# Attention stage: VectorE's instructions kept in the order in which the program issues them

## Chip, cores and metric

One core of a Trainium2 chip (trn2). The time is the device time of one execution in microseconds (us), as the median of several runs; all other times are from one execution that the hardware profiler recorded.

## What is computed

The kernel runs two blocks, one behind the other, on x of shape (1, 512, 1024) in float32. The first mixes a gated MLP branch and a chunked linear recurrence and ends with a feed-forward; the second has a short-convolution mixer with a feed-forward, then attention with another feed-forward. The change is in the attention: 16 heads of 64, 512 positions, causal, with a forget gate whose cumulative sum c is added to the scores. Cut to what matters:

```python
kvf = h @ w_kvf
k = rmsnorm_2(k_s, k_norm)                  # per head
c = cumsum(log_sigmoid(f_logit))
qg = xn @ b_w_qg[j]
q = rmsnorm_2(qg[..., :d], q_norm[j])       # per head
s = q . k + c[q] - c[k], causal             # 64 wide
o = softmax(s) @ v
o = o * sigmoid(qg[..., d:])
x = x + o @ b_w_out[j]
```

## The kernel before

Activations lie as eight tiles of 128 features by 512 positions. Every float32 product is split: each operand has a rounded part h and a remainder l, and three matmuls are summed (xh by wh at L207, xl by wh at L211, xh by wl at L212). A weight chunk is loaded raw by SyncE's queue, and `prep` (L173) makes wh on ScalarE (a cast, L183) and wl on VectorE (L184) up to two chunks ahead of use.

The order on each engine is made by a scheduler from its own estimate of times, not by the program: an instruction moves ahead of others that wait. Only an instruction given to `keep_in_program_order` (short name `pin`, L68) keeps its place among its engine's instructions; before the change those are a few matmuls and the first wl.

The attention stage runs two generators side by side, `weave(main(), side(), *ATT, late=True)` (L1462), which takes steps from one or the other by the amount of matmul work that each has issued. Four of the eight pairs of heads have their query's product issued before that.

- `main()` follows `ORDER = "gqgqgqgqgggg"`: each q is `query(i)`, a product of eight matmul triples and the start of a `HeadNorm`; each g is `gate(i)`: a product, then gz on VectorE (a multiplication by the norm factor rb, then a maximum with -80), then `clamp_sig` on ScalarE (e, e, sg: Exp, Ln, Exp). `paced` calls `finish_norms` and `start_norms` at the fourth and seventh step of each product.
- `HeadNorm.sums` (called by `start_norms`) sums squares on TensorE (L1224, L1225, into hn), then issues in this order: hm on VectorE; Ln and Exp into hr on ScalarE; hn times the gain times hr, on VectorE (L109); then hr by hr and hm by hr, on VectorE for the first four queries and on GpSimd for the later ones (`by`). `out` (called by `finish_norms`) ends it with one more instruction on VectorE.
- `side()` goes through 32 steps, eight pairs of heads by four row blocks tb of 128. A step issues `scores` (TensorE into sc, then two maxima nmx on VectorE, L1366), `shares` of the step before (rs, a reciprocal on VectorE, L1381, then pe times rs for both heads of the pair, L113, on GpSimd for tb 0 and 1, on VectorE for tb 2 and 3), `turn` of two steps before (transposes of pe into pt on TensorE, L1390, and a copy to et on ScalarE), `powers` (pe by Exp with a running sum, on ScalarE), and parts of `stack` (kh, kl, qh, ql of the next pair). Once all four row blocks of a pair are turned, `values` (ao on TensorE, L1403) and og, the gated output, follow a step later. `split` then makes xh and xl of og for the output product.

The lines that matter for the order within a HeadNorm:

```python
ts(dve, self.m, ps, 1.0 / 64, ALU.mult, EPS, ALU.add)
r = T("hr")
f(r, self.m, AF.Ln)
f(r, r, AF.Exp, scale=-0.5)
stt(self.t, self.t, self.gk, r, ALU.mult, ALU.mult)
```

Of the kernel before, what the change touches and what calls it, by code (L numbers as in the profile page):

```python
# [55 lines left out]
@with_exitstack  # L56
def tile_two_blocks(ctx: ExitStack, tc: tile.TileContext, a: dict, out: bass.AP):
    nc = tc.nc
    act, dve, pool, pe = nc.scalar, nc.vector, nc.gpsimd, nc.tensor

    cp = ctx.enter_context(tc.tile_pool(name="const", bufs=1))
    rawp = ctx.enter_context(tc.tile_pool(name="raw", bufs=N_RAW))
# [27 lines left out]
    def close_x():  # L90
        xp[0].close()
# [122 lines left out]
    def mm_T(key, X, m=128):  # L214
        wh, wl = W(key)
        ps = PS("mm")
        nk = len(X)
        o = ps[:m, :]
        for k in range(nk):
            mm3(o, wh[:, k, :], wl[:, k, :], X[k][0], X[k][1], k == 0, k == nk - 1)  # L220
            yield 650
        return ps
# [34 lines left out]
    def run(gen):  # L257
        try:
            while True:
                next(gen)  # L260
        except StopIteration as e:
            return e.value

    def weave(main, side, mt, st, late=False):

        m = s = 0.0
        end = object()
        md = sd = False
        while not (md and sd):
            c = None  # L270
            if not sd and (md or s * mt < m * st or late and not s):
                c = next(side, end)
                if c is end:
                    sd = True
                    continue
                if c is not None:
                    s += c
                    continue
                assert not md
            c = next(main, end)  # L280
            if c is end:
                md = True
            elif s or not late:
                m += c
# [206 lines left out]
    class Acc:  # L491
        def __init__(self):
            self.t = None
# [11 lines left out]
    def split(src, g=None, alloc=None):  # L505
        h, l = (alloc or R)("xh"), (alloc or R)("xl")
        if g is None:
            act.copy(h, src)  # L508
            tt(dve, l, src, h.bitcast(F32), ALU.subtract)
        else:  # L510
            f(h, src, AF.Copy, scale=g)
            stt(l, src, g, h.bitcast(F32), ALU.mult, ALU.subtract)
        return h, l
# [153 lines left out]
    def zi_half(c):  # L667
        pss = yield from mm_N("zi", X)
        for j in range(NT):
            v[j][c] = T("v")  # L670
            f(v[j][c], pss[j], AF.Copy, scale=rcol[:, j:j + 1])

    def head_in(h):
        kq, sc = T2("kq"), T2("sc")
        p = yield from mm_T("zf", X)
        t = T("zf")
        tt(dve, t, p, rb)
        e = T("e")
        f(e, t, AF.Abs)
        f(e, e, AF.Exp, scale=-1.0)  # L680
        f(e, e, AF.Ln, bias=1.0)
        g = T("g")
        stt(g, t, 0.0, e, ALU.min, ALU.subtract)
        dve.tensor_tensor_scan(out=sc[:, 1, :], data0=reset, data1=g, initial=0.0, op0=ALU.mult, op1=ALU.add)  # L684
        stt(e, t, 0.0, e, ALU.max, ALU.add)

        tt(pool, sc[:, 0, :], sc[:, 1, :], e, ALU.add)
        f(kq[:, 0, :], e, AF.Exp, scale=-1.0)
        p = yield from mm_T("zq", X)
        silu(p, kq[:, 1, :])  # L690
        heads[h] = (kq, sc)

    def gate_in(h):
        gate = T("gate")
        p = yield from mm_T("zo", X)
        silu(p, gate, hgs)
        gates[h] = gate
# [175 lines left out]
    def side():  # L873
        cores = {}
        ahead = [0]

        def look(upto):
            while ahead[0] < min(upto, 72):
                h, n = divmod(ahead[0], 9)
                if h not in cores:  # L880
                    if h not in heads:
                        return
                    cores[h] = Core(h)
                cores[h].decays(n)
                ahead[0] += 1

        for h in range(8):
            look(9 * h + 1)
            while h not in cores:
                yield None  # L890
                look(9 * h + 1)
            c = cores[h]
            look(9 * h + 5)
            if h == 0:
                for _ in range(HGSTART):
                    yield None
            c.small()
            look(9 * h + 9)
            yield 2000
            if h:  # L900
                cores[h - 1].values()
                cores[h - 1].square()
                yield 2200
            c.mid()
            yield 800
            if h:
                cores[h - 1].norm()
                yield 500
            c.far()
            look(9 * h + 9 + AHEAD)  # L910
            yield 2000
            if h:
                cores.pop(h - 1).done()
        cores[7].values()
        yield 1000
        cores[7].square()
        yield 1000
        cores[7].norm()
        yield 1000
        cores[7].done()  # L920
# [11 lines left out]
    def main():  # L932
        yield from zi_half(1)
        for h in range(1, 8):
            yield from head_in(h)
            yield from gate_in(h - 1)
        rest.extend(split(t) for t in YF)
        yield from gate_in(7)
        for i in range(N_FILL):
            yield from mix_a(i, rest)  # L940

    def mix_a(i, YA):
        pg = yield from mm_T("ga", X)
        py = yield from mm_T("ua", YA)
        t = T("m1")
        gated(pg, py, t)
        M1.append(t)
# [344 lines left out]
    def paced(mm):  # L1292

        n = 0
        while True:
            try:
                c = next(mm)
            except StopIteration as e:
                return e.value
            n += 1  # L1300
            if n == FIN:
                finish_norms()
            if n == START:
                start_norms()
            yield c

    def query(i):
        p = yield from paced(mm_T("qq", XQ))
        held.append((i, HeadNorm(p, kqs[:, 1:2], act if i < QL else pool)))
# [149 lines left out]
    turns = {"q": QL, "g": 0}  # L1459
    for i in range(QL):  # L1460
        run(query(i))
    weave(main(), side(), *ATT, late=True)  # L1462
    close_x()
    acc = Acc()
    X = [residual("bo", OS, i, V("ffn2", 8 + i), acc) for i in range(8)]
# [27 lines left out]
```

## Time and profile before

| | us |
|---|---|
| runs | 2096.36, 2099.39, 2098.18; median 2098.18 |
| profiled execution, its own time | 2099.46 |
| its span | 2097.7 |
| TensorE matmuls busy (PE) | 2054.9 (98%) |
| TensorE weight loads (PEld) | 1687.0 (80%) |
| VectorE (DVE) | 1180.5 (56%) |
| ScalarE (ACT) | 898.6 (43%) |
| GpSimd (POOL) | 466.4 (22%) |
| scores side by side with gates, from and to | about 1534 to 1690 of the span |

The span runs from the first to the last instruction; the execution's own time is 1.8 us longer. Busy times are of the whole span, so they say which engine is nearly always at work, and not what a single stage waits for; that is in the timelines of its stretch.

### The profile page before, as it was taken

How to read it: one execution, taken by the hardware profiler on the slowest of the kernel's cores; microseconds unless marked ns; L12 is line 12 of the kernel's file. 1: busy time of each engine (PE TensorE's matmuls, PEld its weight loads, DVE VectorE, ACT ScalarE, POOL GpSimd, SP SyncE). 2: the span in 40 equal slices, each digit the busy share in tenths (PEclk: the TensorE clock that was granted, in tenths of full speed). 3: DMA queues.
4: the chain of work that ended last, by engine and by line, in shares of the span. 5: the costliest groups of instructions: out<-in, count | busy, mean ns of one | idle time of the engine just before them, and what ended most of it. 6: DMA issues, size and time to landing. Idle time of an engine off the chain costs nothing.

```text
span 2097.7 us, 27515 instructions
## 1 busy us (share of the span) xinstructions
PE 2054.9 (98%) x11314; PEld 1687.0 (80%) x11314; DVE 1180.5 (56%) x1525; ACT 898.6 (43%) x1444; POOL 466.4 (22%) x421
## 2 busy tenths in 40 slices
PE   8999889999999999999999999999999999999999
PEld 7877678888888888888888888877877778888887
DVE  4678785555444443664654453567577566445353
ACT  5467675543322323522343232345566554323232
POOL 3546661012222222410210000120024211001000
PEclk9999999999999999999999999999999999999999
DMA  7131112323232233323333223241311113323221
GB/s 223 61 101 45 59 61 81 112 90 101 84 117 83 98 101 96 105 70 111 101 101 101 95 88 99 81 122 61 101 41 61 41 61 101 101 84 117 81 92 50
DMA packets 179190, 187.55 MB, mean 89 GB/s; under 512 B 4379, under 2 KB 169976, under 8 KB 179064
## 3 DMA queue, kind: packets, MB, share of 16 engines
q1 hardware_dynamic: 179048, 185.79, 27.4%
q8 instruction: 89, 1.46, 0.3%
q14 instruction: 37, 0.30, 0.0%
q10 hardware_dynamic: 16, 0.00, 0.0%
HBM read 183.68 MB, written 2.10 MB: 89 GB/s over the span
## 4 chain that ended last, share of the span: by engine, by line
PE 88%; DVE 4%; POOL 4%; ACT 2%; issue 1%; DMA 0%; SPq 0%; POOLq 0%; DVEq 0%; ACTq 0%
PE mm L207 26%; PE mm L211 26%; PE mm L212 26%; POOL dec L106 3%; PE mn L252 2%; PE mn L251 2%; PE mn L250 2%; PE sc L1354 1%; PE ao L1403 1%; DVE dec L106 1%; ACT e L119 1%; PE pt L1390 1%; PE ml L237 1%; PE ml L236 1%; PE ml L235 1%
## 5 line engine op out<-in xcount | busy, mean ns | idle before, releaser
L207 PE MATMUL mm<-xh,wh 128*128 128x512 f32 x2544 | 1001.9, 395 | 0.6 <-ACT xh L508 0.6
L211 PE MATMUL mm<-xl,wh 128*128 128x512 f32 x2544 | 993.9, 391 | 0.0
L212 PE MATMUL mm<-xh,wl 128*128 128x512 f32 x2544 | 992.8, 391 | 0.0
L183 ACT CAST wh<-raw 128x1024 fp32r<-128x1024 f32 (+2 forms) x354 | 363.8, 1028 | 787.5 <-PE mm L211 696.5
L184 DVE TENSOR_TENSOR wl<-raw,wh 128x1024 fp32r<-128x1024 f32 (+2 forms) x354 | 462.7, 1308 | 176.4 <-ACT wh L183 174.5
L207 PEld LDWEIGHTS mm<-xh,wh 128*128 128x128 f32 x2544 | 479.7, 189 | 102.3 <-ACT xh L508 0.8
L212 PEld LDWEIGHTS mm<-xh,wl 128*128 128x128 f32 x2544 | 479.4, 188 | 101.0 <-issue 0.2
L211 PEld LDWEIGHTS mm<-xl,wh 128*128 128x128 f32 x2544 | 479.7, 189 | 98.4 <-issue 0.3
L106 POOL TENSOR_TENSOR ua<-ua,rb 128x512 f32<-128x512 f32 x44 | 57.6, 1310 | 589.4 <-ACT ua L119 589.4
L106 DVE TENSOR_TENSOR x<-mm,x 128x512 f32<-128x512 f32 x64 | 44.2, 691 | 154.5 <-PE mm L212 154.5
L106 POOL TENSOR_TENSOR dec<-sc 128x256 f32<-128x256 f32 x96 | 78.8, 851 | 82.4 <-DVE sc L684 82.0
L106 POOL TENSOR_TENSOR acc<-acc,sq 128x512 f32<-128x512 f32 x42 | 67.0, 1596 | 105.0 <-ACT sq L119 77.9
L106 DVE TENSOR_TENSOR a<-mm,rb 128x512 f32<-128x512 f32 x44 | 30.4, 691 | 101.9 <-PE mm L212 101.6
L106 DVE TENSOR_TENSOR sg<-mm,ua 128x512 f32<-128x512 f32 x44 | 30.4, 692 | 92.6 <-POOL ua L106 90.1
L106 POOL TENSOR_TENSOR rl<-rl 128x512 f32<-128x512 f32 x32 | 48.1, 1502 | 117.0 <-ACT rl L119 117.0
L109 DVE SCALAR_TENSOR_TENSOR ua<-a,convs,ua 128x511 f32<-128x511 f32 x88 | 65.8, 748 | 4.7 <-ACT ua L119 3.2
L113 POOL TENSOR_SCALAR pe<-pe,rs 128x128 f32<-128x128 f32 (+1 forms) x32 | 29.6, 937 | 164.7 <-DVE rs L1381 160.5
L119 ACT ACTIVATE ua<-ua 128x512 f32<-128x512 f32 x44 | 27.8, 632 | 85.9 <-DVE ua L109 85.8
L250 PE MATMUL mn<-wh,xh 128*128 128x512 f32 x160 | 62.7, 398 | 0.0
L251 PE MATMUL mn<-wl,xh 128*128 128x512 f32 x160 | 62.4, 390 | 0.0
L252 PE MATMUL mn<-wh,xl 128*128 128x512 f32 x160 | 60.7, 390 | 0.0
L109 DVE SCALAR_TENSOR_TENSOR xl<-x,vecs,xh 128x512 fp32r<-128x512 f32 x40 | 56.1, 1404 | 4.2 <-ACT xh L119 4.0
(279 smaller groups left out, 1838.5 us busy)
## 6 DMA issues: line engine op xcount, KB each, us to landing
raw<-in_ffn_w_up_dram SPq DMA_DIRECT2D x44, 1024.0 KB
raw<-in_w_ff_dram SPq DMA_DIRECT2D x32, 1024.0 KB
raw<-in_w_in_dram SPq DMA_DIRECT2D x26, 1024.0 KB
raw<-in_ffn_w_down_dram SPq DMA_DIRECT2D x18, 1024.0 KB
raw<-in_a_w_in_dram SPq DMA_DIRECT2D x12, 1024.0 KB
raw<-in_w_kvf_dram SPq DMA_DIRECT2D x8, 1024.0 KB
raw<-in_b_w_qg_dram SPq DMA_DIRECT2D x8, 1024.0 KB
raw<-in_w_up_b_dram SPq DMA_DIRECT2D x4, 1024.0 KB
```

The costliest lines, as they stand in the source:

```text
L106: e.tensor_tensor(out=o, in0=i0, in1=i1, op=op)
L109: dve.scalar_tensor_tensor(out=o, in0=i0, scalar=s, in1=i1, op0=op0, op1=op1)
L113: e.tensor_scalar(out=o, in0=i, scalar1=s1, scalar2=None, op0=op0)
L119: act.activation(out=o, in_=i, func=func, scale=scale, bias=bias, **kw)
L183: act.copy(hi, src)
L184: ins = dve.tensor_tensor(out=lo, in0=src, in1=hi.bitcast(F32), op=ALU.subtract)
L207: ins = pe.matmul(ps, lhsT=lh, rhs=rh, start=start, stop=False)
L211: pe.matmul(ps, lhsT=lh, rhs=rl, start=False, stop=False)
L212: pe.matmul(ps, lhsT=ll, rhs=rh, start=False, stop=stop_)
L250: pe.matmul(pss[j], lhsT=xh[:, t0], rhs=wh[:, kk, :], start=(k + kk == 0), stop=False)
L251: pe.matmul(pss[j], lhsT=xh[:, t0], rhs=wl[:, kk, :], start=False, stop=False)
L252: pe.matmul(pss[j], lhsT=xl[:, t0], rhs=wh[:, kk, :], start=False, stop=(k + kk == nk - 1))
```

## The change

Four engines are wrapped in a class that passes every call on and, while an engine is in the set `strict`, gives the instruction to `keep_in_program_order`. VectorE (`dve`) is put into the set before the weave, and the set is emptied after it. All instructions and their operands stay as they are. In the orders below, every call through the wrapper has the line L70 in the changed kernel.

```diff
--- before.py
+++ after.py
@@ -56,7 +56,25 @@
 @with_exitstack
 def tile_two_blocks(ctx: ExitStack, tc: tile.TileContext, a: dict, out: bass.AP):
     nc = tc.nc
-    act, dve, pool, pe = nc.scalar, nc.vector, nc.gpsimd, nc.tensor
+
+    strict = set()
+
+    class InOrder:
+        def __init__(self, engine):
+            self.engine = engine
+
+        def __getattr__(self, name):
+            call = getattr(self.engine, name)
+
+            def issue(*args, **kw):
+                ins = call(*args, **kw)
+                if self in strict and name != "dma_start":
+                    tc.keep_in_program_order(ins)
+                return ins
+
+            return issue
+
+    act, dve, pool, pe = (InOrder(e) for e in (nc.scalar, nc.vector, nc.gpsimd, nc.tensor))
 
     cp = ctx.enter_context(tc.tile_pool(name="const", bufs=1))
     rawp = ctx.enter_context(tc.tile_pool(name="raw", bufs=N_RAW))
@@ -1459,7 +1477,9 @@
     turns = {"q": QL, "g": 0}
     for i in range(QL):
         run(query(i))
+    strict.add(dve)
     weave(main(), side(), *ATT, late=True)
+    strict.clear()
     close_x()
     acc = Acc()
     X = [residual("bo", OS, i, V("ffn2", 8 + i), acc) for i in range(8)]
```

How this moves VectorE's instructions is shown at three places. A row has the line, the operation, the output with its allocation numbers, the operands and the shape; the numbers tell tiles of one name apart.

VectorE around query 3 (hm_2078_12133 is its HeadNorm, gz_2083 and wl_2087 belong to a gate, nmx_2082 and nmx_2098 to scores, rs_2099 to shares), before:

```order
L115 TENSOR_SCALAR hm_2078_12133<-hn_2077_12130 128x512
L106 TENSOR_TENSOR gz_2083_12161<-mm_2076_12107,rb_1890_11221 128x512
L106 TENSOR_TENSOR kl_2095_12185<-hn_1905_11286,kh_2093_12183 128x512
L1366 TENSOR_REDUCE nmx_2098_12202<-sc_2096_12188 128x1
L1366 TENSOR_REDUCE nmx_2098_12202<-sc_2097_12189 128x1
L113 TENSOR_SCALAR gz_2083_12161<-gz_2083_12161 128x512
L1381 RECIPROCAL rs_2099_12208<-sum_2089_12177 128x2
```

The same place in the changed kernel, from the row behind hm_2078_12133:

```order
L70 SCALAR_TENSOR_TENSOR hn_2066_12087<-hn_2066_12087,kqs_11140,hr_2079_12135 128x512
L70 TENSOR_TENSOR hr_2079_12135<-hr_2079_12135 128x512
L70 TENSOR_TENSOR hm_2078_12133<-hm_2078_12133,hr_2079_12135 128x512
L70 TENSOR_REDUCE nmx_2082_12158<-sc_2080_12144 128x1
L70 TENSOR_REDUCE nmx_2082_12158<-sc_2081_12145 128x1
L70 TENSOR_TENSOR gz_2083_12161<-mm_2076_12107,rb_1890_11221 128x512
L70 TENSOR_SCALAR gz_2083_12161<-gz_2083_12161 128x512
L70 TENSOR_TENSOR wl_2087_12170<-raw_2059_12044,wh_2086_12169 128x1024
L70 TENSOR_TENSOR kl_2095_12185<-hn_1905_11286,kh_2093_12183 128x512
L70 TENSOR_REDUCE nmx_2098_12202<-sc_2096_12188 128x1
L70 TENSOR_REDUCE nmx_2098_12202<-sc_2097_12189 128x1
L70 RECIPROCAL rs_2099_12208<-sum_2089_12177 128x2
```

hn_2066 with its operand hr_2079, and the two multiplications behind it, now stand directly behind hm_2078 (they stood behind wl_2087 and later rows), and rs_2099 comes behind them and behind wl_2087.

VectorE around query 4 (hm_2173 and hn_2148 are its HeadNorm; rs_2185 and pe_2168, pe_2169 are shares), before:

```order
L1381 RECIPROCAL rs_2185_12536<-sum_2167_12447 128x2
L115 TENSOR_SCALAR hm_2173_12490<-hn_2172_12487 128x512
L1366 TENSOR_REDUCE nmx_2177_12512<-sc_2176_12499 128x1
L113 TENSOR_SCALAR pe_2168_12448<-pe_2168_12448,rs_2185_12536 128x384
L113 TENSOR_SCALAR pe_2169_12450<-pe_2169_12450,rs_2185_12536 128x384
L106 TENSOR_TENSOR gz_2178_12518<-mm_2155_12401,rb_1890_11221 128x512
L184 TENSOR_TENSOR wl_2183_12529<-raw_2181_12526,wh_2182_12528 128x1024
L1366 TENSOR_REDUCE nmx_2195_12569<-sc_2193_12555 128x1
L1366 TENSOR_REDUCE nmx_2195_12569<-sc_2194_12556 128x1
L113 TENSOR_SCALAR gz_2178_12518<-gz_2178_12518 128x512
L1381 RECIPROCAL rs_2196_12575<-sum_2190_12550 128x2
L109 SCALAR_TENSOR_TENSOR hn_2148_12387<-hn_2148_12387,kqs_11140,hr_2174_12492 128x512
```

And in the changed kernel:

```order
L70 TENSOR_SCALAR hm_2173_12490<-hn_2172_12487 128x512
L70 SCALAR_TENSOR_TENSOR hn_2148_12387<-hn_2148_12387,kqs_11140,hr_2174_12492 128x512
L70 TENSOR_REDUCE nmx_2177_12512<-sc_2175_12498 128x1
L70 TENSOR_REDUCE nmx_2177_12512<-sc_2176_12499 128x1
L70 TENSOR_TENSOR gz_2178_12518<-mm_2155_12401,rb_1890_11221 128x512
L70 TENSOR_SCALAR gz_2178_12518<-gz_2178_12518 128x512
L70 TENSOR_TENSOR wl_2183_12529<-raw_2181_12526,wh_2182_12528 128x1024
L70 RECIPROCAL rs_2185_12536<-sum_2167_12447 128x2
L70 TENSOR_SCALAR pe_2168_12448<-pe_2168_12448,rs_2185_12536 128x384
L70 TENSOR_SCALAR pe_2169_12450<-pe_2169_12450,rs_2185_12536 128x384
```

hn_2148 moves from the end of the piece to the place behind hm_2173; rs_2185 and its two pe, once at the head, now stand at the end, behind a gate and wl_2183.

VectorE around query 6 (hm_2356 and hn_2306 are its HeadNorm, og_2364 a gated output, rs_2368 and pe_2352, pe_2353 shares), before:

```order
L115 TENSOR_SCALAR hm_2356_13201<-hn_2355_13198 128x512
L106 TENSOR_TENSOR gz_2358_13212<-mm_2313_13030,rb_1890_11221 128x512
L113 TENSOR_SCALAR gz_2358_13212<-gz_2358_13212 128x512
L184 TENSOR_TENSOR wl_2362_13221<-raw_2310_13024,wh_2361_13220 128x1024
L109 SCALAR_TENSOR_TENSOR hn_2306_13016<-hn_2306_13016,kqs_11140,hr_2357_13203 128x512
L1366 TENSOR_REDUCE nmx_2367_13247<-sc_2365_13233 128x1
L1366 TENSOR_REDUCE nmx_2367_13247<-sc_2366_13234 128x1
L1381 RECIPROCAL rs_2368_13257<-sum_2351_13169 128x2
L106 TENSOR_TENSOR og_2364_13228<-ao_2354_13174,sg_2360_13218 128x512
L113 TENSOR_SCALAR pe_2352_13170<-pe_2352_13170,rs_2368_13257 128x384
L113 TENSOR_SCALAR pe_2353_13172<-pe_2353_13172,rs_2368_13257 128x384
```

And in the changed kernel:

```order
L70 TENSOR_SCALAR hm_2356_13201<-hn_2355_13198 128x512
L70 SCALAR_TENSOR_TENSOR hn_2306_13016<-hn_2306_13016,kqs_11140,hr_2357_13203 128x512
L70 TENSOR_TENSOR gz_2358_13212<-mm_2313_13030,rb_1890_11221 128x512
L70 TENSOR_SCALAR gz_2358_13212<-gz_2358_13212 128x512
L70 TENSOR_TENSOR wl_2362_13221<-raw_2310_13024,wh_2361_13220 128x1024
L70 TENSOR_TENSOR og_2364_13228<-ao_2354_13174,sg_2360_13218 128x512
L70 TENSOR_REDUCE nmx_2367_13247<-sc_2365_13233 128x1
L70 TENSOR_REDUCE nmx_2367_13247<-sc_2366_13234 128x1
L70 SCALAR_TENSOR_TENSOR hn_2306_13016<-hm_2356_13201,hn_2306_13016 128x512
L70 RECIPROCAL rs_2368_13257<-sum_2351_13169 128x2
L70 TENSOR_SCALAR pe_2352_13170<-pe_2352_13170,rs_2368_13257 128x384
L70 TENSOR_SCALAR pe_2353_13172<-pe_2353_13172,rs_2368_13257 128x384
```

hn_2306 moves directly behind hm_2356, og_2364 ahead of the maxima nmx_2367, and the second hn_2306 ahead of rs_2368. At query 7 the rows move in the same way. On GpSimd, at query 5, hr_2260_12828 and hm_2259_12826 stand ahead of pe_2262_12835 and pe_2263_12837; before, behind them. At one of the last gates VectorE has wl_14078 ahead of that gate's second gz, before behind it.

## Rows read from the trace of the kernel before

**Rows 1.** Timeline of TensorE: start, duration, instructions, count [idle time before <- what ended it].

```profile
1542.22 0.33 PE L1390 MATMUL pt<-ident,pe 128*128 128x128 f32 x1 [0.65 <-POOL pe L113]
1543.34 0.33 PE L1390 MATMUL pt<-ident,pe 128*128 128x128 f32 x1 [0.79 <-POOL pe L113]
...
1568.33 0.82 PE L1390 MATMUL pt<-ident,pe 128*128 128x128 f32 x6
...
1593.96 0.38 PE L1390 MATMUL pt<-ident,pe 128*128 128x128 f32 x2
...
1622.38 0.84 PE L1390 MATMUL pt<-ident,pe 128*128 128x128 f32 x6 [0.22 <-DVE pe L113]
...
1642.82 0.88 PE L1390 MATMUL pt<-ident,pe 128*128 128x128 f32 x3 [2.56 <-DVE pe L113]
1644.15 0.88 PE L1390 MATMUL pt<-ident,pe 128*128 128x128 f32 x3 [0.47 <-DVE rs L1381]
...
1682.34 1.07 PE L1390 MATMUL pt<-ident,pe 128*128 128x128 f32 x8 [1.46 <-DVE pe L113]
...
1685.47 0.97 PE L207 MATMUL mm<-xh,wh 128*128 128x512 f32 x3 [0.61 <-ACT xh L508]
```

**Rows 2.** Timeline of VectorE at query 3.

```profile
1537.51 0.69 DVE L115 TENSOR_SCALAR hm<-hn 128x512 f32<-128x512 f32 x1 [0.55 <-PE hn L1225]
1538.21 0.69 DVE L106 TENSOR_TENSOR gz<-mm,rb 128x512 f32<-128x512 f32 x1
1538.82 0.68 DVE L106 TENSOR_TENSOR kl<-hn,kh 128x512 fp32r<-128x512 f32 x1
1539.41 0.75 DVE L1366 TENSOR_REDUCE nmx<-sc 128x1 f32<-128x256 f32 x2
1540.08 0.42 DVE L113 TENSOR_SCALAR gz<-gz 128x512 f32<-128x512 f32 x1
1540.41 0.16 DVE L1381 RECIPROCAL rs<-sum 128x2 f32<-128x2 f32 x1
1540.49 1.21 DVE L184 TENSOR_TENSOR wl<-raw,wh 128x1024 fp32r<-128x1024 f32 x1
...
1542.07 0.74 DVE L109 SCALAR_TENSOR_TENSOR hn<-hn,kqs,hr 128x512 f32<-128x512 f32 x1
```

**Rows 3.** Timeline of VectorE at queries 4 and 6.

```profile
1565.96 0.74 DVE L113 TENSOR_SCALAR pe<-pe,rs 128x384 f32<-128x384 f32 x2
...
1619.38 1.28 DVE L1366 TENSOR_REDUCE nmx<-sc 128x1 f32<-128x512 f32 x2
```

**Rows 4.** Timeline of ScalarE: Ln of queries 4, 6 and 7, Exp of query 5.

```profile
1566.44 0.63 ACT L119 ACTIVATE hr<-hm 128x512 f32<-128x512 f32 x1
...
1590.49 0.63 ACT L119 ACTIVATE hr<-hr 128x512 f32<-128x512 f32 x1
...
1616.92 0.62 ACT L119 ACTIVATE hr<-hm 128x512 f32<-128x512 f32 x1
...
1637.86 0.62 ACT L119 ACTIVATE hr<-hm 128x512 f32<-128x512 f32 x1
```

**Rows 5.** Timeline of GpSimd at queries 5 and 7.

```profile
1590.78 1.66 POOL L113 TENSOR_SCALAR pe<-pe,rs 128x128 f32<-128x128 f32 x2 [6.13 <-DVE rs L1381]
1592.41 1.03 POOL L106 TENSOR_TENSOR hr<-hr 128x512 f32<-128x512 f32 x1
...
1642.48 1.31 POOL L106 TENSOR_TENSOR hm<-hm,hr 128x512 f32<-128x512 f32 x1
```

**Rows 6.** Stretches: length, busy time of PE, PEld, DVE, ACT, POOL, granted clock, DMA, GB/s.

```profile
1542.00:1550.00 8.00, 6.99 (x42) 4.98 (x43) 5.94 (x14) 5.02 (x15) 4.07 (x4) 0.79 0.41 131
1640.00:1650.00 10.00, 6.97 (x36) 5.09 (x35) 6.21 (x15) 4.66 (x15) 2.35 (x2) 0.66 0.31 105
1680.00:1690.00 10.00, 7.91 (x66) 5.91 (x67) 5.77 (x11) 9.12 (x18) 0.00 (x0) 1.00 0.01 2
```

## The prediction

> **What bounds the kernel now.** I read the table of busy times first: TensorE is busy 98% of the span, so only what makes TensorE stand still, or slows its clock, can move the time. Outside the stretch from 1443 to 1690 us the two programs are row for row the same, and up to 1534 us the moved rows (weight remainders wl, past some key norms) are used 9 us or more after the place where they now stand, which covers a delay of one or two instructions. So the change is decided between 1534 and 1690 us, where scores and gates run side by side. The second view is TensorE's timeline there [rows 1]. The reader should see what ends its idle times: nearly always pe, the softmax shares that the transposes pt read. They come from VectorE, or from GpSimd for row blocks 0 and 1, behind rs on VectorE. So the question is how early rs and pe stand in VectorE's queue. Third come the rows of VectorE, ScalarE and GpSimd around those places [rows 2 to 5], and last the granted clock of the stretches with idle TensorE [rows 6].
>
> **What the change does there.** It removes and adds no instruction and no transfer; SyncE's order is the same, and so are GpSimd's rows but for seven places. VectorE now takes its instructions as written. The price is one pattern, five times (queries 3 to 7): start_norms writes hm, then two activations of ScalarE (Ln, Exp), then hn, which needs their result hr. The scheduler had put gates, maxima, rs and pe between hm and hn; as written, hn stands directly behind hm, VectorE waits for both activations, and rs and pe, written later, wait behind it. I walk each place with the durations of before. An instruction that doesn't wait for the last one starts about 0.08 us before its printed end (gz 0.69, next start 0.61 later [rows 2]), one that does takes its full time.
>
> **A, query 3.** Before, rs ended at 1540.57 [rows 2], and the transposes of GpSimd's two pe came 1.65 and 2.77 us behind it [rows 1]. After: hm, with a kl of 0.68 ahead of it, 1538.2 to 1538.9; Ln and Exp 0.63 and 0.62 [rows 4], 1540.15; hn 0.74, and hr and hm as multiplications of 0.69, each waiting for the last, 1542.3; the first two maxima nmx, 0.4 by an estimate from the wider pair, 1542.7; gz 0.61 and 0.34, wl 1.13, kl 0.59, nmx pair 0.67, rs 0.16 [rows 2], 3.5 together: 1546.2. Transposes at 1547.85 instead of 1542.22: **+5.6**.
>
> **B, query 4.** hm is early (1564.5 to 1565.2) but Ln stands behind a weight cast and ran at 1566.44 [rows 4]; I take 1566.3, Exp ends at 1567.5. hn 1568.2, nmx pair of 512 columns 1.2 [rows 3] 1569.4, gz pair 0.95, wl 1.13, rs 0.16, the first pe 0.37 [rows 3]: 1572.0, instead of 1568.33 [rows 1]: **+3.7**.
>
> **Query 5.** On VectorE nothing awaited moves back, but on GpSimd hr and hm now come ahead of two pe. Exp ends at 1591.12 [rows 4], hn 1591.9, hr 1.03, hm 1.31, two pe 1.66 [rows 5]: 1595.9 or, with starts between engines, 1596.1, instead of 1593.96 [rows 1]: **+2.1**.
>
> **C, query 6.** Here og, which needs the gate's sg, also stands ahead of the maxima. Ln starts at 1616.92 and Exp ends at 1618.15 [rows 4]; hn 1618.9; gz pair 1.03, 1619.95; e, e, sg on ScalarE at 0.63 each, 1621.85 (wl lies beside them); og 0.65, nmx 1.2, hn 0.65, rs 0.16, first pe 0.4: 1624.95, instead of 1622.38 [rows 1]: **+2.6**.
>
> **D, query 7.** The same chain from Ln at 1637.86 [rows 4] ends at 1645.2. Before, the second transposes waited again, until 1644.15 [rows 1], with pe beside GpSimd's hm of 1.31 [rows 5]; now GpSimd has finished by then, and they follow at 1645.6: **+1.45**.
>
> **E, the tail.** wl goes ahead of the gate's second instruction (1.13), and xh, which waits on that gate, lets TensorE go on at 1686.6 instead of 1685.47 [rows 1]: **+1.15**.
>
> Score matmuls of a few blocks change between interleaved and sequential pairs; TensorE has as many of either, so I put it at 0 (bounds 0.5 either way). The stalls sum to **+16.6**. They add up because TensorE works without a pause between the places, so a delay at one shifts the next whole.
>
> **The clock.** Before, the idle times at A (0.65 and 0.79) and D (2.56 and 0.47) [rows 1] were followed by stretches at the lower level, 1.2 instead of 2.4 GHz: the mean granted clock of 0.79 over 8 us [rows 6] is 3.4 us at half, or 1.7 us lost; 0.66 over 10 us is 6.8 us at half, at most 3.4 lost, of which I take 3.0 since some of it was idle anyway. A and D pay that already. B and C had next to none (0.22 at C [rows 1]), and now get 3.7 and 2.6, more than A had. Bounds for each from these rows: 0 to 3.0; I take the middle of the two prices, 2.35 each, **+4.7**. Query 5 and E I take at 0: E had 1.46 and 0.61 idle [rows 1], and the clock stayed at 1.00 [rows 6]. The whole clock term lies between 0 and 10.7 (3.0 at B and at C, 1.7 each at query 5 and E, 1.3 more at A).
>
> The Trainium skill speaks against part of this: its page "TensorE: Matmul & The Clock Gate", section "HAM oscillation — how this bites in real kernels", has the clock fall back behind long waits between groups of matmuls, not behind short ones. By it the terms at B and C would go, and the sum be 16.6. A's row disagrees, E's agrees.
>
> **Sum:** 16.6 + 4.7 = +21.3. The profiled execution took 2099.46 us, its span 2097.7; the median of the runs is 1.28 us below it. 2099.46 + 21.3 - 1.28 = **2119.5 us**.
>
> **Rivals.**
> - *Stalls without new slow stretches* (the page's rule as a mechanism here): TensorE gets gaps of 2 to 4 us at B and C, as at E, and stays at full clock. For it speaks E, against it A. +16.6, 2114.8 us. Chance 0.20.
> - *Only A costs.* Shares are issued a step before their transposes, so a later VectorE could be made up by blocks of scores in between, once TensorE has been shifted by A. Against it: the idle times that remain after A before (2.56 at D) show that one step is no reserve. +5.6, 2103.8 us. Chance 0.12.
> - *Larger clock.* All terms at the upper bound: 16.6 + 10.7 = +27.3, 2125.5 us. Chance 0.10.
> - *Faster: the awaited rs and pe come sooner.* Before, the scheduler put work of younger steps ahead of them at A and D. If the written order takes more of it away than the wait for hr adds, the idle times 0.65 + 0.79 + 2.56 + 0.47 and the lower clock there, 1.7 + 3.0, are gained: at most -9.2, 2089.0 us. It decides from the point where the younger work ahead of rs exceeds Ln, Exp and hn, 2.0 us. At D I find one such instruction, of about 0.4. Chance 0.05.
> - *No effect*, if the wrapper reached no instruction: the orders of VectorE differ at 83 places, so only if every move were covered. 2098.2 us. Chance 0.03.
>
> **How the numbers follow.** The forecast has the remaining 0.50. The walk is good to a quarter of its stalls, 4 us, since it takes ScalarE's order as it was. The range reaches from the case where only A costs, 2103, to the larger clock with some of that error, 2128; outside are faster and no effect, and the ends of the walk. A measurement here tells 0.2%, 4.2 us, from no change: faster 0.05, same 0.04 (no effect, and the low end of only A), slower 0.91.
>
> **What would show it.** In the profile after, VectorE's hn (kqs, hr) should be preceded by idle time that ends with ScalarE's hr, at five places, above all at A, B and C; TensorE's pt rows should wait about 6 to 7 us in all at A, about 4 at B, 2 at query 5, 3 at C and 4 at D; and the 156 us between the first scores and the last values should become about 177. Right in mechanism and wrong in size if the waits are there and the clock at B and C stays 1.00. Wrong if hn's waits are there but no pt behind them gets idle time (slack covers them), or if TensorE's idle time grows at places with no HeadNorm near: then the written order costs elsewhere, and I have missed it.

## The result, and the profile after

The changed kernel takes 2124.05 us (median of 4 runs, 2123.99 to 2126.08), the kernel before 2098.78 in the same comparison (4 runs): ratio 1.0125, 95% interval 1.0109 to 1.0141, 25.3 us slower. 2119.5 us had been forecast, with a range of 2103 to 2128. The profiled execution is the slowest of the four: 2126.08 us, span 2124.4, against 2099.46 and 2097.7 before; between the profiles lie 26.7 us of span.

TensorE's timeline of the changed kernel, with the same columns as [rows 1]:

```profile
1547.33 1.06 PE L70 MATMUL pt<-ident,pe 128*128 128x128 f32 x2 [5.32 <-POOL pe L70]
...
1578.69 1.54 PE L70 MATMUL pt<-ident,pe 128*128 128x128 f32 x6 [4.44 <-DVE pe L70]
...
1610.47 0.33 PE L70 MATMUL pt<-ident,pe 128*128 128x128 f32 x1 [2.57 <-POOL pe L70]
1611.25 0.33 PE L70 MATMUL pt<-ident,pe 128*128 128x128 f32 x1 [0.45 <-POOL pe L70]
1612.33 3.89 PE L70 MATMUL ao<-et,v 128*64 128x128 f32 x40
...
1644.62 1.51 PE L70 MATMUL pt<-ident,pe 128*128 128x128 f32 x6 [3.37 <-DVE pe L70]
...
1670.53 1.51 PE L70 MATMUL pt<-ident,pe 128*128 128x128 f32 x6 [4.69 <-DVE pe L70]
...
1712.10 0.96 PE L70 MATMUL mm<-xh,wh 128*128 128x512 f32 x3 [2.34 <-ACT xh L70]
```

From top to bottom these are query 3, 4, 5 (three rows), 6, 7 and the tail. At the five queries TensorE waits for the shares pe, at the tail for xh, at the places that the walk named. The sums of all waits of TensorE from 1530 to 1720 us, of the changed kernel (us in total, times, longest):

```profile
PE pt L70 <- DVE pe L70: 13.3, 4, 4.7
PE pt L70 <- POOL pe L70: 8.3, 3, 5.3
PE mm L70 <- ACT xh L70: 2.3, 1, 2.3
PE sc L70 <- DVE gz L70: 0.4, 1, 0.4
```

That is 24.3 us. In the kernel before the same view gives:

```profile
PE pt L1390 <- DVE pe L113: 4.2, 3, 2.6
PE pt L1390 <- POOL pe L113: 1.4, 2, 0.8
PE mm L207 <- ACT xh L508: 0.6, 1, 0.6
PE pt L1390 <- DVE rs L1381: 0.5, 1, 0.5
PE pt L1390 <- ACT pe L119: 0.5, 2, 0.3
```

7.2 us: the waits grew by 17.1 us, and 9.6 us of the 26.7 are something else. Why pe comes late stands in VectorE's timeline of the changed kernel, hm and hn of the five HeadNorms:

```profile
1538.25 0.69 DVE L70 TENSOR_SCALAR hm<-hn 128x512 f32<-128x512 f32 x1
1540.35 0.75 DVE L70 SCALAR_TENSOR_TENSOR hn<-hn,kqs,hr 128x512 f32<-128x512 f32 x1 [1.42 <-ACT hr L70]
...
1546.33 0.15 DVE L70 RECIPROCAL rs<-sum 128x2 f32<-128x2 f32 x1
...
1570.28 0.69 DVE L70 TENSOR_SCALAR hm<-hn 128x512 f32<-128x512 f32 x1 [3.68 <-PE hn L70]
1573.41 0.75 DVE L70 SCALAR_TENSOR_TENSOR hn<-hn,kqs,hr 128x512 f32<-128x512 f32 x1 [2.44 <-ACT hr L70]
...
1602.82 0.69 DVE L70 TENSOR_SCALAR hm<-hn 128x512 f32<-128x512 f32 x1 [1.25 <-PE hn L70]
1605.00 0.75 DVE L70 SCALAR_TENSOR_TENSOR hn<-hn,kqs,hr 128x512 f32<-128x512 f32 x1 [1.49 <-ACT hr L70]
...
1634.34 0.69 DVE L70 TENSOR_SCALAR hm<-hn 128x512 f32<-128x512 f32 x1 [1.22 <-PE hn L70]
1637.15 0.75 DVE L70 SCALAR_TENSOR_TENSOR hn<-hn,kqs,hr 128x512 f32<-128x512 f32 x1 [2.12 <-ACT hr L70]
...
1660.89 0.69 DVE L70 TENSOR_SCALAR hm<-hn 128x512 f32<-128x512 f32 x1 [5.46 <-PE hn L70]
1663.70 0.75 DVE L70 SCALAR_TENSOR_TENSOR hn<-hn,kqs,hr 128x512 f32<-128x512 f32 x1 [2.12 <-ACT hr L70]
```

Five times hn stands still for ScalarE's hr, 1.4 to 2.4 us, and rs and pe wait behind it in VectorE's queue. (At query 5 the awaited pe are GpSimd's; there they stand behind hr and hm, which need hn.) rs at query 3 started at 1546.33; the walk had its end at 1546.2, and before it started at 1540.41 [rows 2].

These hm rows are good marks, because they follow TensorE's sums of squares at once. Before, they start at 1537.51 [rows 2] and at:

```profile
1529.49 0.69 DVE L115 TENSOR_SCALAR hm<-hn 128x512 f32<-128x512 f32 x1 [0.35 <-PE hn L1225]
...
1564.78 0.67 DVE L115 TENSOR_SCALAR hm<-hn 128x512 f32<-128x512 f32 x1
...
1589.04 0.69 DVE L115 TENSOR_SCALAR hm<-hn 128x512 f32<-128x512 f32 x1 [0.30 <-PE hn L1225]
...
1615.50 0.69 DVE L115 TENSOR_SCALAR hm<-hn 128x512 f32<-128x512 f32 x1 [1.94 <-PE hn L1225]
...
1636.44 0.69 DVE L115 TENSOR_SCALAR hm<-hn 128x512 f32<-128x512 f32 x1 [6.23 <-PE hn L1225]
...
1689.43 0.69 DVE L106 TENSOR_TENSOR og<-ao,sg 128x512 f32<-128x512 f32 x1 [1.21 <-PE ao L1403]
```

In the changed kernel the first and last of these marks (hm of query 2, the last og) are at 1529.53 and 1716.07. So between marks the change cost: around query 3 (first mark to hm of query 4) 40.75 instead of 35.29, +5.46; query 4 +8.28; query 5 +5.06; query 6 +5.61; query 7 and the tail together +2.19; all 26.60. All of the loss lies in this stretch.

The rest beside the waits is TensorE's clock. Windows behind query 3, 4, 5, 6, 7 and at the tail, columns as in [rows 6]:

```profile
1547.00:1557.00 10.00, 9.56 (x50) 6.69 (x50) 5.80 (x15) 5.63 (x20) 2.68 (x4) 0.65 0.28 94
1578.00:1590.00 12.00, 11.31 (x53) 8.84 (x54) 6.12 (x17) 6.58 (x19) 1.46 (x2) 0.58 0.01 1
1612.00:1622.00 10.00, 10.00 (x75) 8.07 (x74) 2.83 (x6) 1.51 (x4) 1.74 (x2) 0.83 0.26 90
1644.00:1654.00 10.00, 9.38 (x54) 7.39 (x55) 5.73 (x16) 6.64 (x20) 1.19 (x2) 0.72 0.21 74
1670.00:1680.00 10.00, 9.47 (x67) 7.59 (x69) 5.36 (x15) 5.75 (x20) 1.18 (x2) 0.83 0.26 91
1704.00:1716.00 12.00, 8.82 (x73) 6.33 (x72) 6.80 (x14) 10.04 (x21) 0.00 (x0) 1.00 0.01 1
```

Behind each of the five HeadNorms TensorE ran for a while at 1.2 instead of 2.4 GHz, at the tail not. The 3.89 us of the 40 ao matmuls at query 5, where before they took 2.40, is the same fact in a single row. The kernel before had such stretches only at queries 3 and 7 (0.79 and 0.66 [rows 6]). So between the marks TensorE was busy longer by 1.47, 4.10, 2.04 and 2.46 us at queries 3 to 6 and shorter by 0.79 at query 7 with the tail, 9.3 us in all, with the same number of matmuls in each piece (to within one).

### The profile page after: what moved, and what is told of

The parts are those of the page before. It is cut to its first block, busy times and chain, and to the rows that moved or that the text cites. A ratio compares the mean times of both kernels' runs of the same rounds, so it can differ in the third digit from the quotient of the medians.

```text
span 2124.4 us, 27507 instructions
## 1 busy us (share of the span) xinstructions
PE 2064.3 (97%) x11314; PEld 1694.6 (80%) x11314; DVE 1182.0 (56%) x1525; ACT 902.5 (42%) x1444; POOL 463.7 (22%) x421
## 3 DMA queue, kind: packets, MB, share of 16 engines
q8 instruction: 89, 1.46, 0.3%
## 4 chain that ended last, share of the span: by engine, by line
PE 87%; DVE 5%; POOL 4%; ACT 2%; issue 1%; DMA 0%; SPq 0%; POOLq 0%; DVEq 0%; ACTq 0%
PE mm L70 76%; PE mn L70 5%; POOL dec L70 3%; PE ml L70 2%; PE sc L70 1%; PE ao L70 1%; PE pt L70 1%; DVE wl L70 1%; DVE dec L70 1%; ACT e L70 1%; DVE sc L70 1%; ACT dec L70 0%; POOL sc L70 0%; ACT wh L70 0%; ACT hr L70 0%
## 5 line engine op out<-in xcount | busy, mean ns | idle before, releaser
L70 PE MATMUL mm<-xh,wh 128*128 128x512 f32 x2544 | 1003.7, 395 | 2.3 <-ACT xh L70 2.3
L70 PE MATMUL mm<-xl,wh 128*128 128x512 f32 x2544 | 994.5, 391 | 0.0
L70 PE MATMUL mm<-xh,wl 128*128 128x512 f32 x2544 | 993.9, 391 | 0.0
L70 ACT CAST wh<-raw 128x1024 fp32r<-128x1024 f32 (+2 forms) x354 | 363.8, 1028 | 805.1 <-PE mm L70 712.5
L70 PEld LDWEIGHTS mm<-xh,wh 128*128 128x128 f32 x2544 | 480.5, 189 | 104.2 <-ACT xh L70 2.6
L70 DVE TENSOR_TENSOR wl<-raw,wh 128x1024 fp32r<-128x1024 f32 (+2 forms) x354 | 464.8, 1314 | 173.1 <-ACT wh L70 169.7
L70 PEld LDWEIGHTS mm<-xh,wl 128*128 128x128 f32 x2544 | 480.0, 189 | 101.3 <-issue 0.2
L70 PEld LDWEIGHTS mm<-xl,wh 128*128 128x128 f32 x2544 | 480.4, 189 | 98.0 <-issue 0.2
L70 POOL TENSOR_TENSOR ua<-ua,rb 128x512 f32<-128x512 f32 x44 | 57.7, 1310 | 589.4 <-ACT ua L70 589.4
L70 DVE TENSOR_TENSOR x<-mm,x 128x512 f32<-128x512 f32 x64 | 44.2, 691 | 154.5 <-PE mm L70 154.5
L70 POOL TENSOR_TENSOR dec<-sc 128x256 f32<-128x256 f32 x96 | 78.8, 851 | 82.4 <-DVE sc L70 81.9
L70 POOL TENSOR_TENSOR acc<-acc,sq 128x512 f32<-128x512 f32 x42 | 67.0, 1596 | 105.0 <-ACT sq L70 77.8
L70 DVE TENSOR_TENSOR a<-mm,rb 128x512 f32<-128x512 f32 x44 | 30.4, 691 | 102.0 <-PE mm L70 101.8
L70 DVE TENSOR_TENSOR sg<-mm,ua 128x512 f32<-128x512 f32 x44 | 30.4, 692 | 92.4 <-POOL ua L70 90.0
L70 POOL TENSOR_TENSOR rl<-rl 128x512 f32<-128x512 f32 x32 | 48.1, 1503 | 117.0 <-ACT rl L70 117.0
L70 DVE SCALAR_TENSOR_TENSOR ua<-a,convs,ua 128x511 f32<-128x511 f32 x88 | 65.8, 748 | 4.7 <-ACT ua L70 3.2
L70 POOL TENSOR_SCALAR pe<-pe,rs 128x128 f32<-128x128 f32 (+1 forms) x32 | 26.6, 842 | 186.5 <-DVE rs L70 164.5
L70 ACT ACTIVATE ua<-ua 128x512 f32<-128x512 f32 x44 | 27.8, 632 | 85.9 <-DVE ua L70 85.8
L70 PE MATMUL mn<-wh,xh 128*128 128x512 f32 x160 | 62.7, 399 | 0.0
L70 PE MATMUL mn<-wl,xh 128*128 128x512 f32 x160 | 62.4, 390 | 0.0
L70 PE MATMUL mn<-wh,xl 128*128 128x512 f32 x160 | 60.7, 389 | 0.0
L70 DVE SCALAR_TENSOR_TENSOR xl<-x,vecs,xh 128x512 fp32r<-128x512 f32 x40 | 55.9, 1404 | 4.1 <-ACT xh L70 4.0
```

Source lines behind the costliest of these rows:

```text
L70: ins = call(*args, **kw)
```

## The experiments

Every kernel was compared with runs of the kernel before on its own chip; times are medians. The theory to test had two parts: what counts is how much the written order puts ahead of rs and pe on VectorE (the wait for hr, and the work that is queued behind it), and TensorE's lower clock comes on top.

**Is it the wait for hr alone?** The first kernel issues what follows Exp in a HeadNorm later, at the second step of the next product.

```diff
-            stt(self.t, self.t, self.gk, r, ALU.mult, ALU.mult)
+            self.r = r
+
+        def scale(self):
+            r = self.r
+            stt(self.t, self.t, self.gk, r, ALU.mult, ALU.mult)
...
+    MID = 2
...
+            if n == MID:
+                for _, hn in summed:
+                    hn.scale()
             if n == FIN:
```

> The changed kernel, with the three instructions of a HeadNorm that follow ScalarE's Exp issued some three matmul triples later, so that VectorE should no longer stand still for hr. Theory 1, the wait for ScalarE at the head of VectorE's queue is the whole cost: the five waits of the transposes vanish and the time is within 4 us of before, 2097 to 2103 us. Theory 2, what counts is everything that the written order puts ahead of rs and pe, the wait being one item of it: by the walk about +4.4 at query 3 (hn, hr, hm, a weight remainder, kl and the maxima still stand ahead of rs), +0.7 at query 4, 0 at query 5, +1.2 at query 6, -0.3 at query 7, +1.15 at the tail, 7 us of waits and up to 2 for the clock at query 3: 2106 to 2109 us.

Measured 2111.22 us, ratio 1.0061 (1.0044 to 1.0078), +13.1 us. Between the marks, from query 3 to 6 and then query 7 with the tail: +4.5, +1.4, 0.0, +4.2, +1.3. The wait for hr is gone and about half of the loss stays, so theory 1 falls: at query 3 most of it is the work ahead of rs. Theory 2's range, 2106 to 2109, is missed too, by 2 us: queries 3, 4, 5 and the rest came out within 0.7 us of its terms, query 6 did not (+1.2 expected). There the wait only changed its place, as VectorE's timeline shows:

```profile
1624.59 0.69 DVE L70 TENSOR_TENSOR og<-ao,sg 128x512 f32<-128x512 f32 x1 [1.33 <-ACT sg L70]
...
1628.50 0.69 DVE L70 SCALAR_TENSOR_TENSOR hn<-hm,hn 128x512 f32<-128x512 f32 x1 [1.36 <-POOL hm L70]
1629.11 0.15 DVE L70 RECIPROCAL rs<-sum 128x2 f32<-128x2 f32 x1
```

og waits for sg as before, and the HeadNorm's last instruction, which stands ahead of rs, now waits for GpSimd's hm, since GpSimd overwrites hr and so comes behind the late hn.

**Shares ahead of scores.** The second kernel moves one line, the third has both edits.

```diff
+            if sums:
+                shares()
             if n < 32:
                 ps, nmx = scores(i, tb)
                 yield 100 + 214 * (tb + 1)
-            if sums:
-                shares()
```

> The changed kernel, with a step's shares (rs and pe) issued ahead of its scores instead of behind them; the HeadNorms as in the changed kernel, VectorE still waits for hr. Theory 1 (the wait for hr alone): rs and pe still stand behind hn, so little is gained, 2118 to 2124 us. Theory 2 (everything ahead of rs and pe): +4.9 at query 3, +0.4 at query 4, +2 to 3 at query 5, +0.7 at query 6, +0.3 at query 7, some 9 us of waits, and 2 to 4 for the clock at queries 3 and 5: 2108 to 2113 us.

Measured 2121.74 us, 1.0110 (1.0095 to 1.0125), +23.6 us; between the marks +4.1, +5.4, +4.3, +5.1, +3.1. (In this kernel and the next, six score matmuls, about 0.5 us, come behind the mark of query 4 instead of ahead of it, so query 3 looks that much better and query 4 worse than they are.) The number is theory 1's; theory 2's is missed by 9 us, most of all at queries 4 and 6, where it had +0.4 and +0.7. At query 4 VectorE's two pe started directly behind hn, but took 2.63 us (see the last section), and the transposes still waited when they were done. TensorE's row:

```profile
1576.67 1.54 PE L70 MATMUL pt<-ident,pe 128*128 128x128 f32 x6 [3.46 <-ACT pe L70]
```

The wait is ended by ScalarE's powers of the newest block of scores, whose maxima now stand behind hn, rs and pe on VectorE. That fits a tile pt that gets the bank which those scores leave; it wasn't tried apart. At query 6 TensorE waits 1.61 us for pe and 0.84 for GpSimd's hsl, and it is busy 2.9 us longer than before. So while VectorE's queue is blocked, a better order behind the blocked instruction gains little, since the transposes need more than one thing from there.

> Both edits together: the HeadNorm's last three instructions later, and shares ahead of scores. Theory 1: as with the later HeadNorm alone, 2097 to 2103 us. Theory 2: +1.6 at query 3, nothing at queries 4 to 6, -1.4 at query 7, where the kernel before has a wait of its own, +1.15 at the tail; with the clock of query 7 partly regained 2095 to 2101 us, and clearly less than with the later HeadNorm alone.

Measured 2103.93 us, 1.0029 (1.0018 to 1.0040), +5.8 us; +0.8, +0.7, 0.0, +2.1, +4.1. With the wait for hr gone and rs and pe first, queries 3 to 5 together are within 1.5 us of before. Theory 2's 2095 to 2101 is still missed by 3 us, and theory 1's 2097 to 2103 by 1. The later HeadNorm alone gained 13 us, shares first alone 2, both 20: wait and work are not two sums but one queue, and at queries 3 to 5 they carry the loss together. Query 7, where a gain was expected, still loses: the HeadNorm's last instruction waited 2.58 us for GpSimd's hm, again in front of rs.

**One place alone.** Two kernels keep VectorE's order only around one query (the engine enters the set at a step of the scores and leaves it at another): query 5 (steps 11 to 14) and query 4 (6 to 8).

```diff
+            if n == 11:
+                strict.add(dve)
+            if n == 14:
+                strict.clear()
...
-    strict.add(dve)
     weave(main(), side(), *ATT, late=True)
```

> VectorE's order kept as issued only from step 11 to step 14 of the scores, around query 5; everywhere else the order of before. If places add up and each is priced by what stands there, this costs what the changed kernel's trace shows between its marks at queries 5 and 6, 5.1 us (3.0 of waits, the rest the lower clock): 2102 to 2104 us. If the prediction's term were right and the rest of the 5.1 were left over from queries 3 and 4: +2.1, 2099.5 to 2101 us. If a later slack absorbs a single place: 2097 to 2099 us.

Measured 2103.01 us, 1.0029 (1.0018 to 1.0041), +6.0 us. Between the marks around query 5 +5.08, against +5.06 in the changed kernel; at query 3, where nothing is pinned, -1.6 (see the last section), then 0.0, 0.0 and -0.4 at queries 4, 6 and behind.

> The same around query 4 alone (steps 6 to 8 of the scores). Additive and priced by the place: the 8.3 us that the changed kernel's trace shows between its marks at queries 4 and 5, of which 4.2 are waits, and up to 1.5 more because the HeadNorm's last instruction, which waits for GpSimd, here comes ahead of pe: 2105 to 2108 us. If a single place is absorbed by later slack: 2097 to 2100 us.

Measured 2104.77 us, 1.0040 (1.0026 to 1.0054), +7.8 us, just below the expected 2105, and between its marks +8.24 against +8.28; no later piece gained more than 0.3 us. So places add up and none is absorbed later: two places alone reproduce their shares of the loss. That the match is 0.04 us at query 4 is partly chance, since the HeadNorm's last instruction comes ahead of pe in this kernel and the wait is longer (4.91 us instead of 4.44), while TensorE's busy time grew by 3.6 us instead of 4.1:

```profile
1570.63 1.54 PE L70 MATMUL pt<-ident,pe 128*128 128x128 f32 x6 [4.91 <-DVE pe L70]
```

That ends the rival in which only query 3 costs.

**The clock.** Dummy matmuls fill TensorE's waits, so that it is never idle for long; they write the pt tile ahead of its transposes.

```diff
+    FILL = {0: 20, 6: 16, 12: 10, 18: 12, 22: 18}
...
+        if h % 2 == 0:
+            n = h // 2 * 4 + tb
+            for _ in range(FILL.get(n, 0)):
+                pe.matmul(pt, lhsT=bones, rhs=stacks[(n + LAG) // 4][0], start=True, stop=True)
```

> The changed kernel, with dummy matmuls (20, 16, 10, 12 and 18 of 512 columns, into the tile that the next transposes overwrite) where TensorE waits at queries 3 to 7; each set is shorter than the wait in which it stands. Theory (TensorE's lower clock behind its idle times costs what the sum of waits, 17.1 us in the two traces, leaves of the 26.7 us between their spans): the granted clock stays at 1.00 behind the filled places, and the time falls by the 9.6 us, and by up to 4.7 us more that the kernel before pays at queries 3 and 7 too: 2109 to 2115 us. Rival (the rest is not the clock but matmuls in another order): the time stays, 2122 to 2127 us.

Measured 2121.78 us, 1.0111 (1.0096 to 1.0126): only 2 us below the changed kernel, far from the 2109 to 2115 of the theory and next to the rival's 2122. Between the marks the filling saved 2.3, 1.9, 1.6 and 2.2 us at queries 3 to 6, and lost 2.8 behind. At query 7 its 18 matmuls started late, at the lower clock, and took longer than the wait:

```profile
1659.22 6.83 PE L70 MATMUL pt<-qh,bones 128*128 128x512 f32 x18 [2.31 <-ACT et L70]
```

So the second filling leaves query 7 out (`FILL = {0: 18, 6: 12, 12: 10, 18: 12}`).

> The changed kernel with dummy matmuls at queries 3 to 6 only (18, 12, 10, 12), none at query 7, where the first filling ran at the lower clock and was longer than its wait. Clock theory: between its marks the first filling took 2.3, 1.9, 1.6 and 2.2 us less than the changed kernel at queries 3 to 6 and 2.8 more behind; without the latter the time should fall by 8 us from 2124, to 2115 to 2118 us. Rival, no net gain from a higher clock: 2121 to 2125 us.

Measured 2118.75 us, 1.0104 (1.0091 to 1.0118), just above the expected 2115 to 2118: 5.3 us less than the changed kernel by the medians, 3.5 if each is taken against its own runs of before (+21.74 and +25.27), 7.0 by the two profiled executions (2119.12 and 2126.08). Windows behind queries 4, 5 and 6 of this kernel:

```profile
1580.00:1590.00 10.00, 10.00 (x91) 7.95 (x90) 3.97 (x10) 5.42 (x16) 3.01 (x4) 1.00 0.00 0
1612.00:1622.00 10.00, 10.00 (x63) 7.54 (x62) 6.05 (x14) 4.72 (x14) 3.02 (x2) 1.00 0.00 0
1640.00:1650.00 10.00, 10.00 (x67) 7.64 (x68) 5.99 (x14) 7.05 (x20) 3.38 (x4) 1.00 0.10 34
```

Behind these three the clock stayed at 1.00 where it had been 0.58 to 0.83, and the time fell though work was added. The clock is thus a real part of the loss, some 4 to 7 us of it for four places, shown by taking it away. The filling is not a clean measure: it waited itself at queries 3 and 4, 1.29 us until ScalarE's pe and 1.77 until VectorE's gz (presumably for the bank of its tile), and TensorE ran part of those two fillings at the lower clock. So how much of the whole 9.3 us it would give back stays open.

**More of the suspected wait.** One more activation, a copy of hr onto itself, between Exp and hn.

```diff
             f(r, r, AF.Exp, scale=-0.5)
+            if strict:
+                act.copy(r, r)
```

> The changed kernel with one more activation of ScalarE, an in-place copy of hr of about 0.6 us, between each HeadNorm's Exp and hn, for the five HeadNorms of the side-by-side stretch. If hr is what VectorE waits for and rs and pe wait behind it, all five places grow by 0.6: about 3 us over the changed kernel, 2126 to 2129 us, and hn's idle time grows by 0.6 to about 2.0, 3.0, 2.1, 2.7 and 2.7. If only the order of the work counts and the wait is covered: no change, 2123 to 2125 us.

Measured 2132.74 us, 1.0163 (1.0146 to 1.0180), 8.7 us over the changed kernel where 3 were expected. hn's idle time grew as said at four places, to 2.07, 3.10, 2.77 and 2.77 us, and at query 5 to 2.94 instead of 2.1. TensorE's waits sum to 28.3 us, 4.0 more, and at each place they grew by what hn's did (0.65, 0.66, 1.28, 0.63 and 0.66 us, the last in front of scores that wait for gz). So the wait for hr is on the path at every place. What it cost there is uneven: against the changed kernel +0.3, +0.3, +2.5 and +0.5 between the marks of queries 3 to 6 and +3.4 behind. The difference is the clock: TensorE was busy 1.2 us longer at query 5 and 2.7 longer at query 7 and the tail, where the 10 us that begin half a us before the awaited transposes have 0.69 (0.83 in the changed kernel), and up to 0.4 shorter at the other three.

**A version that beats both.** If early rs and pe are what counts, the scheduler can be helped without pinning anything: the kernel before, with shares issued ahead of scores.

> The kernel before with nothing pinned, and one edit: a step's shares issued ahead of its scores. The scheduler then puts rs and pe ahead of hm at queries 4, 6 and 7 and right behind it at query 3. If the place of rs and pe in VectorE's queue is what counts: the waits of before at query 3 (0.65 + 0.79) and 7 (2.56 + 0.47) and the lower clock behind them (1.7 + 3.0) go, up to -9.2: 2089 to 2094 us. If banks of PSUM or ScalarE's powers are next at once: 2096 to 2099 us.

Measured 2093.99 us (11 runs) against 2097.01 (17 runs), ratio 0.9986 (0.9977 to 0.9995): 3.0 us faster than before and 30 us faster than the changed kernel, at the slow end of the 2089 to 2094 expected. All waits of TensorE in the stretch:

```profile
PE mm L207 <- ACT xh L508: 2.2, 1, 2.2
PE pt L1390 <- ACT pe L119: 1.2, 1, 1.2
PE sc L1354 <- ACT pe L119: 1.1, 1, 1.1
PE pt L1390 <- DVE pe L113: 0.6, 1, 0.6
```

5.1 us instead of 7.2; those of queries 3 and 7 shrank from 4.5 to 1.7, and new ones came at query 4 (1.1, with 0.83 as the clock from 1570 to 1580 us) and at the tail (2.2). Between the marks: -3.7 around query 3, +3.7 around query 4, -5.1 at query 7 and the tail. About 1.2 us of the first two is the mark alone: 11 score matmuls that stood ahead of hm of query 4 now follow it. The marks sum to -5.5, the spans of the two profiles differ by 3.5: this profile had lost 1.9 us ahead of the first mark, which was not traced further.

## Why the prediction was right

It held in direction and mechanism, and the time lies within the range: 25.3 us by the medians where 21.3 were forecast. The signs that it named came: hn waits for hr at five places, and pt behind it 5.3, 4.4, 3.0, 3.4 and 4.7 us (6 to 7, 4, 2, 3 and 4 had been named). By its own terms, against the marks of the profiled executions:

| term | forecast, waits + clock | measured between marks | growth of TensorE's waits | growth of its busy time |
|---|---|---|---|---|
| A, query 3 | 5.6 + 0 | 5.46 | 3.88 | 1.47 |
| B, query 4 | 3.7 + 2.35 | 8.28 | 4.18 | 4.10 |
| query 5 | 2.1 + 0 | 5.06 | 3.02 | 2.04 |
| C, query 6 | 2.6 + 2.35 | 5.61 | 3.15 | 2.46 |
| D and E, query 7 and tail | 2.6 + 0 | 2.19 | 2.98 | -0.79 |
| sum | 16.6 + 4.7 | 26.60 | 17.2 | 9.3 |

- **The walk** along VectorE's new order held: 17.2 us of waits (the rows added up) instead of 16.6. That the sum is so close is partly luck: A was 1.7 us too high, the other rows together 2.3 too low. GpSimd's pe at queries 3 and 5 had other lengths than before:

```profile
1546.66 1.20 POOL L70 TENSOR_SCALAR pe<-pe,rs 128x128 f32<-128x128 f32 x2 [120.75 <-DVE rs L70]
...
1607.33 1.28 POOL L70 TENSOR_TENSOR hm<-hm,hr 128x512 f32<-128x512 f32 x1
1608.59 2.60 POOL L70 TENSOR_SCALAR pe<-pe,rs 128x128 f32<-128x128 f32 x2
```

At A both were done 1.53 us after rs started; the walk had taken 1.65 and 2.77 us behind rs for the transposes from [rows 1], so the waits there were shorter, and the lower clock made up the rest: A's 5.6 against 5.46 is luck. It also leans on the run of before, which paid 1.7 us of clock at this place that other runs did not pay (last section). At query 5 it was the other way, 2.60 us instead of 1.66 [rows 5]; whether VectorE's work beside them made them long was not tried apart.
- **The clock** is the term that was mis-sized: 4.7 forecast, 9.3 measured by the table's last column. The step that failed is that query 5 was taken at 0, by E's row: 2.57 and 0.45 us of waits were followed by the lower clock (0.83 over 10 us) in the changed kernel, and again (0.83) where query 5 stood alone. At B the price was 4.1 us, not 2.35, and A, which was to have paid already, paid 1.5 more. The bounds of 0 to 10.7 for the whole clock term held, but not the bounds of its parts: 3.0 at B, 1.7 at query 5 and 1.3 at A were all passed, and query 7 with the tail gave 0.8 back.
- The rule weighed there, of the Trainium skill, "TensorE: Matmul & The Clock Gate", section "HAM oscillation — how this bites in real kernels", is one of long waits; the prediction took it to clear both B and C, which gives 16.6 us. The waits in that section's own example are about as long as those of A, B, C and query 7 here (5.32, 4.44, 3.37 and 4.69 us, each with the lower clock behind it), so these rows agree with it, and it was read wrongly for B. Query 5's row disagrees (2.57 and 0.45 us, then 0.83), the tail's agrees (2.34 us, then 1.00).
- **The rivals:** "only A costs" falls by the two single places. "Stalls without new slow stretches" falls by the windows; it likened gaps of 2 to 4 us to E, whose longest was 1.46. "Faster" never met its condition, since the wait for hr and what follows it adds more at every place than the younger work that goes; but its idea, rs and pe sooner, is what the last kernel turns into a gain. "Larger clock" (27.3 us, 10.7 of them clock) was nearly what came.

## What to carry to other kernels

In these traces VectorE took its instructions one by one: rs and pe did not start before an hn ahead of them that waited for hr. So a written order is good only where no instruction that waits for another engine stands ahead of one that a bound engine is waiting for. When an order is fixed, issue each instruction that ends a chain through another engine (here hm, Ln, Exp, hn) as late as its own reader allows, and what TensorE waits for as early as its data allow. Price a longer gap of TensorE with the clock behind it: here it cost 1.4 to 2.0 times the growth of the waits at queries 3 to 6, and 0.7 times at query 7 and the tail.

## What was not expected of the hardware

The same gaps did not always bring the lower clock. At query 3 the kernel that pins only query 5 has VectorE's order of before and the same waits, 0.64 and 0.80 us, but this window:

```profile
1542.00:1550.00 8.00, 7.02 (x52) 5.09 (x54) 7.17 (x18) 6.20 (x21) 4.04 (x4) 1.00 0.41 131
```

The kernel before had 0.79 there [rows 6], and its stretch up to hm of query 4 was 1.6 us longer; the kernel that pins only query 4 has 1.00 there too and is 1.8 us shorter. So the 1.7 us of clock that the prediction read there are not in every run, and against these two kernels A would have cost 7.0 to 7.3 us instead of 5.46.

VectorE's pe became up to three and a half times longer beside GpSimd: with shares first, two pe of 384 columns took 2.63 us instead of 0.74 [rows 3], while GpSimd's hr and hm (1.04 and 1.26 us) ran from 1572.60 to 1574.98:

```profile
1572.57 2.63 DVE L70 TENSOR_SCALAR pe<-pe,rs 128x384 f32<-128x384 f32 x2
...
1573.72 1.26 POOL L70 TENSOR_TENSOR hm<-hm,hr 128x512 f32<-128x512 f32 x1
```

The eleven traces hold 88 such pairs. The 73 with no GpSimd instruction beside them (0.03 us at most) took 0.73 to 0.75 us, the 15 with one beside them 1.32 to 2.63; no pair was in between.

The Trainium skill, "SBUF — State Buffer", section "Who interferes with whom", says that VectorE in its two-port modes and GpSimd take turns at a shared pair of ports, a whole instruction at a time. These rows agree with it: the pair above ended 0.22 us after GpSimd's hm.
